# Low halves of sixteen weight loads per mixer computed on GpSimd instead of VectorE

## The chip, the cores and the metric

The kernel runs on one core of one Trainium2 chip. The metric is device time in microseconds (us); the time of a kernel is the median of its runs. In the rows of the profile PE is TensorE's matmuls and PEld its weight loads, DVE is VectorE, ACT is ScalarE, POOL is GpSimd, SP is SyncE.

## The reference, cut to what matters

Two layers of a trunk over 640 tokens (128 prompt, 512 sample) with a width of 1024. Each layer is a mixer and then a SwiGLU. The mixer is one projection `h @ w_in` that feeds three groups of heads, then `w_out`:

```python
sc_b, sc_c, sc_h, q, k, v, dn_qkv, dn_z, dn_a, dn_b = jnp.split(h @ p['w_in'], splits, axis=-1)
y_sc = sc_b * _dwconv(sc_c * sc_h, p['sc_conv_w'])
... = attention(q, k, v)
... = delta_mixer(silu(dwconv(dn_qkv)), dn_z, dn_a, dn_b)
y = jnp.concatenate([y_sc, y_att, y_dn], axis=-1) @ p['w_out']
```

The delta mixer inverts a unit lower triangular matrix for each chunk of 64 tokens and then scans over the chunks.

## The kernel before

All products take their operands as a high and a low part. `load_w` (L177) brings a slice of weights from memory into a tile `raw` (three buffers), then `split` (L170) makes two tiles of it: `whi`, a copy rounded to the matmul's type, made by ScalarE (L172), and `wlo = raw - whi`, made by VectorE (L173). Both have two buffers, so that the tiles of a load can be written once the products of the load before the last have read theirs. A product (`fm_product`, L193, and `tm_product`, L608) issues three matmuls for each slice of 128 rows: high by high (L199, L616), high by low (L201, L618), and low by high (L202, L617). The first matmul with `wlo` is thus the second or third of the product. `split` stands under `high_priority`, which lets the program's builder put both halves ahead of other work on their engines as soon as their inputs are there. Each engine then runs its instructions in the order that was fixed when the program was built.

One mixer has, in the order of its loads: two loads made before it begins (`first`), two z tiles of their own (not `whi` and `wlo`), and then sixteen loads of 128x1024 into `whi` and `wlo`: the delta mixer's n4, n5 and n0, the short convolution's c0, the delta mixer's n1, both halves of the first queries (q0a, q0b), the convolution's h0, both halves of the second queries (q1a, q1b), the convolution's b0, c1 and h1, both halves of keys and values (ka, kb), and the convolution's b1. The letters of `SEQ` set the order of the blocks: `n` is a delta mixer projection, `d` a step of the convolution, `q` queries, `k` keys and values, `I` and `J` the inversion of the large group of chunks, `i` that of the small one, `s` a scan step.

The inversion `I` is a loop of 31 steps on VectorE: `tmp <- Ls, Ts` (L999) and `Ts <- Ts, tmp` (L1001). It is followed by transposes on VectorE (L1008 to L1011), copies (`adx`, L1018) and small matmuls (L1025). GpSimd does small things in a mixer: fills, `scp * csb` of the convolution (L1138), the rotary products (L1098) and the scan's `Sd` (L1255).

Of the kernel before, what the change touches and what calls it, by code (L numbers as in the profile page):

```python
# [23 lines left out]
KT_ = 8  # L24
# [84 lines left out]
def hybrid_trunk_kernel(  # L109
# [8 lines left out]
    V, A, G, PE = nc.vector, nc.scalar, nc.gpsimd, nc.tensor  # L118
# [20 lines left out]
    def pmm():  # L139
        return ps.tile([128, 512], F32, tag="mm", name="pmm", bufs=2)  # L140
# [29 lines left out]
    def split(src, hi, lo, hi_eng=None, lo_eng=None):  # L170

        (hi_eng or A.copy)(hi, src)  # L172
        (lo_eng or V).tensor_tensor(out=lo, in0=src, in1=hi.bitcast(F32), op=ALU.subtract)  # L173

    loads = []

    def load_w(src, nk, n, side=None):  # L177
        raw = wp.tile([128, nk, n], F32, tag="raw", name="raw", bufs=RAW_BUFS)
        loads.append(nc.sync.dma_start(out=raw, in_=src))
        if isinstance(side, tuple):  # L180
            hi, lo = side
        elif side is None:
            hi, lo = (wp.tile([128, nk, n], F32R, tag=tag, name=tag, bufs=W_BUFS) for tag in ("whi", "wlo"))
        else:
            hi, lo = (side.tile([128, nk, n], F32R, tag=tag, name=tag, bufs=SIDE_BUFS) for tag in ("xhi", "xlo"))
        with tc.high_priority():
            split(raw, hi, lo)
        return hi, lo

    def wslice(w, k0, nk, c0, n):  # L190
        return w[k0 * 128:(k0 + nk) * 128, c0:c0 + n].rearrange("(k p) n -> p k n", p=128)

    def fm_product(pt, wh, wl, acts, h, lead=False):  # L193

        n = len(acts)
        o = pt[:, 0:HH]
        for k in range(n):
            ah, al = acts[k][h]
            mm(o, lhsT=wh[:, k], rhs=ah, start=k == 0, stop=False)  # L199
            if not lead:  # L200
                mm(o, lhsT=wh[:, k], rhs=al, start=False, stop=False)  # L201
            mm(o, lhsT=wl[:, k], rhs=ah, start=False, stop=not lead and k == n - 1)  # L202
        if lead:
            for k in range(n):
                mm(o, lhsT=wh[:, k], rhs=acts[k][h][1], start=False, stop=k == n - 1)
# [354 lines left out]
    def pieces(h):  # L560

        if h == 0:
            return ((0, 128, 0), (128, HH, 128))
        return ((0, HH, HH),)
# [9 lines left out]
    def padcol(tok):  # L574

        return 1 + tok if tok < 128 else 131 + tok - 128


    def mixer(l, mp, hs, early_half, fill, first, later):
        win = w_in[l]  # L580
# [6 lines left out]
        def cvt(name, shape=(128, 644), dt=F32):  # L587
            return mp.tile(list(shape), dt, tag="cv", name=name, bufs=CV_BUFS)

        def sm(tag, name, n, bufs):  # L590
            return mp.tile([128, n], F32, tag=tag, name=name, bufs=bufs)

        def padded(name):
            p = cvt(name)
            G.memset(p[:, 0:1], 0.0)
            G.memset(p[:, 129:131], 0.0)
            G.memset(p[:, 643:644], 0.0)
            return p

        def conv3(p, w0, w1, w2, name):  # L600
            y = cvt(name, (128, 642))
            A.activation(y, p[:, 0:642], AF.Copy, scale=w0)
            V.scalar_tensor_tensor(out=y, in0=p[:, 1:643], scalar=w1, in1=y, op0=ALU.mult, op1=ALU.add)
            V.scalar_tensor_tensor(out=y, in0=p[:, 2:644], scalar=w2, in1=y, op0=ALU.mult, op1=ALU.add)
            return y
# [4 lines left out]
        def tm_product(pt, ws, t):  # L610

            ts = slice(t * 128, (t + 1) * 128)
            for k in range(KT_):
                wh, wl = ws[k // 4]
                ah, al = hs[k].hi, hs[k].lo
                mm(pt, lhsT=ah[:, ts], rhs=wh[:, k % 4], start=k == 0, stop=False)  # L616
                mm(pt, lhsT=ah[:, ts], rhs=wl[:, k % 4], start=False, stop=False)  # L617
                mm(pt, lhsT=al[:, ts], rhs=wh[:, k % 4], start=False, stop=k == 7)  # L618

        def dn_load(m):  # L620
            return load_w(wslice(win, 0, KT_, 1536 + m * 128, 128), KT_, 128)

        ws = first
        ps_ = [padded("dnp") for _ in ws]
# [495 lines left out]
        ysc = []  # L1120
        def short_conv():
            for m in range(2):
                wc = load_w(wslice(win, 0, KT_, 256 + m * 128, 128), KT_, 128)
                csb = cvt("csb", (128, TOK))
                for h in range(2):
                    pt = pmm()
                    fm_product(pt, wc[0], wc[1], hs, h)
                    A.copy(csb[:, HB[h][0]:HB[h][1]], pt[:, 0:HH])
                yield
                wh_ = load_w(wslice(win, 0, KT_, 512 + m * 128, 128), KT_, 128)  # L1130
                p = padded("scp")
                for h in range(2):
                    pt = pmm()
                    fm_product(pt, wh_[0], wh_[1], hs, h)
                    for a0, a1, tok in pieces(h):
                        pv = p[:, padcol(tok):padcol(tok) + a1 - a0]
                        A.copy(pv, pt[:, a0:a1])
                        G.tensor_tensor(out=pv, in0=pv, in1=csb[:, tok:tok + a1 - a0], op=ALU.mult)  # L1138
                y = conv3(p, vl[:, 64 + m:65 + m], vl[:, 66 + m:67 + m], vl[:, 68 + m:69 + m], "scy")
                yield  # L1140
                wb = load_w(wslice(win, 0, KT_, m * 128, 128), KT_, 128)
                ys = cvt("ysc", (128, TOK))
                for h in range(2):
                    pt = pmm()
                    fm_product(pt, wb[0], wb[1], hs, h)
                    for a0, a1, tok in pieces(h):
                        V.tensor_tensor(out=ys[:, tok:tok + a1 - a0], in0=pt[:, a0:a1],
                                        in1=y[:, padcol(tok) - 1:padcol(tok) - 1 + a1 - a0], op=ALU.mult)
                ysc.append(ys)
                yield  # L1150
# [1 line left out]
        dg = short_conv()  # L1152

        def queries(hb):
            wq = [load_w(wslice(win, kk, 4, 768 + hb * 256, 256), 4, 256) for kk in (0, 4)]
            for t in range(NT):
                pt = pmm()
                tm_product(pt[:, 0:256], wq, t)
                qv = sm("qv", "qv", 256, 2)
                A.copy(qv, pt[:, 0:256])  # L1160
                headss(qv, qss[:, t, hb * 4:hb * 4 + 4], 4)
                nc.scalar.dma_start(out=qscr[t, :, hb * 256:(hb + 1) * 256], in_=qv)
            if hb == 1:
                rsqrt_dve(qss.rearrange("p t h -> p (t h)"), NT * 8, 1.0 / 64, EPS, ((rq.rearrange("p t h -> p (t h)"), lambda y: y, 0.125),), "q")


        def keys():
            kraw = cvt("kraw", (128, NT, 128))
            kvc = sm("qv", "kvc", 256, 2)
            nc.scalar.dma_start(out=kvc[:, 0:128], in_=cache_k[0, l].rearrange("s v d -> s (v d)"))  # L1170
            nc.scalar.dma_start(out=kvc[:, 128:256], in_=cache_v[0, l].rearrange("s v d -> s (v d)"))
            put_keys(kvc[:, 0:128], KTs[:, :, :, 256:384])
            put_values(kvc[:, 128:256], 5)

            wkv = [load_w(wslice(win, kk, 4, 1280, 256), 4, 256) for kk in (0, 4)]
            for t in range(NT):
                pt = pmm()
                tm_product(pt[:, 0:256], wkv, t)
                A.copy(kraw[:, t], pt[:, 0:128])
                if t == 0:  # L1180
                    nv = sm("qv", "nv", 256, 2)
                    A.copy(nv[:, 0:128], pt[:, 128:256])
                    nc.scalar.dma_start(out=new_v[0, l].rearrange("s v d -> s (v d)"), in_=nv[:, 0:128])
                put_values(pt[:, 128:256], t)
                headss(kraw[:, t], kss[:, t], 2)
            rsqrt_dve(kss.rearrange("p t h -> p (t h)"), NT * 2, 1.0 / 64, EPS, ((rk.rearrange("p t h -> p (t h)"), lambda y: y, 1.0),), "k")
            for t in range(NT):
                kn = kraw[:, t]
                scaled(kn, rk[:, t], 2)
                if t == 0:  # L1190
                    gained(kn, 64, 2)
                    nc.scalar.dma_start(out=new_k[0, l].rearrange("s v d -> s (v d)"), in_=kn)
                    put_keys(kn, KTp)
                else:
                    rope(kn, sm("asq", "ktm", 256, 2)[:, 0:128], 1, t, 2)
                    pos = (0, 1, 3, 4)[t - 1]
                    put_keys(kn, KTs[:, :, :, pos * 128:(pos + 1) * 128])
# [680 lines left out]
```

## Time and profile before

| what | value |
|---|---|
| median of 3 runs | 1778.72 us (1776.96 to 1785.07) |
| profiled execution, its own time | 1782.25 us |
| its span, first to last instruction | 1780.5 us |
| busy: PE, DVE, ACT, POOL | 94%, 70%, 44%, 9% of the span |
| granted TensorE clock, mean | 0.974 of full speed |

Busy shares are means over the whole execution. The first mixer lies between about 60 and 400 us, the second between about 925 and 1275 us; what the change touches lies in the first two thirds of each.

### The profile page before, as it was taken

To read this page: it belongs to the slowest core of one execution; us is meant where nothing else is said; L and a number is where in the kernel's file an instruction comes from. 1 tells how busy PE (TensorE), PEld (TensorE's weight loads), DVE (VectorE), ACT (ScalarE), POOL (GpSimd) and SP (SyncE) were. 2 spreads that over 40 slices of the span, in tenths; PEclk is the share of its full clock that TensorE was granted. 3 is DMA by queue.
4 is the path that set the end of the run, shared out by engine and by line. 5 is a ranking of instruction groups with operands and counts; after the bars stand their busy time and mean duration, and the time that the engine had idled before them with its cause. 6 is when DMAs were issued, how large, how long until landed. Compare 5 with 4: busy or idle time off the path is not lost. (4 is left out here: it accounts for less than half of the span.)

```text
span 1780.5 us, 34163 instructions
## 1 busy us (share of the span) xinstructions
PE 1676.7 (94%) x13677; PEld 1497.3 (84%) x13677; DVE 1242.5 (70%) x2764; ACT 782.7 (44%) x1620; POOL 156.3 (9%) x270
## 2 busy tenths in 40 slices
PE   5998999999999999999999989999998999999998
PEld 3887875478899999999988879655888999999998
DVE  3699767665966767666677994886578766667654
ACT  3555244544643433434355442555365343434332
POOL 1111012102300000000032001120041000000000
PEclk8999999999999999999999989999999999999999
DMA  8512224555534223222232222445722222222212
GB/s 280 187 37 78 72 87 129 185 178 164 155 119 131 81 74 96 72 83 73 71 99 75 63 58 67 151 143 164 233 63 84 83 73 82 83 84 84 73 59 60
DMA packets 207693, 188.42 MB, mean 106 GB/s; under 512 B 12782, under 2 KB 182702, under 8 KB 207534
## 3 DMA queue, kind: packets, MB, share of 16 engines
q1 hardware_dynamic: 190656, 170.71, 31.2%
q10 hardware_dynamic: 16878, 15.53, 2.8%
q8 instruction: 108, 1.77, 0.4%
q14 instruction: 51, 0.42, 0.1%
HBM read 168.64 MB, written 17.56 MB: 105 GB/s over the span
## 5 line engine op out<-in xcount | busy, mean ns | idle before, releaser
L172 ACT CAST whi<-raw 128x1024 fp32r<-128x1024 f32 (+1 forms) x102 | 100.0, 981 | 166.5 <-PE pmx L201 73.5
L173 DVE TENSOR_TENSOR wlo<-raw,whi 128x1024 fp32r<-128x1024 f32 (+1 forms) x102 | 115.9, 1138 | 26.5 <-ACT whi L172 26.0
L202 PE MATMUL pmm<-hh,wlo 128*128 128x320 f32 x336 | 109.4, 327 | 6.6 <-DVE wlo L173 6.5
L199 PE MATMUL pmm<-hh,whi 128*128 128x320 f32 x336 | 109.9, 328 | 4.2 <-ACT dnp L645 2.9
L199 PE MATMUL pmm<-acth,whi 128*128 128x320 f32 x320 | 100.6, 314 | 7.3 <-DVE xt L571 7.3
L571 DVE SCALAR_TENSOR_TENSOR xt<-pmx,mod,xt 128x128 f32<-128x128 f32 (+2 forms) x168 | 68.9, 434 | 51.9 <-PE pmx L202 49.5
L201 PE MATMUL pmm<-hl,whi 128*128 128x320 f32 x320 | 104.0, 325 | 0.0
L199 PE MATMUL pmx<-acth,whi 128*128 128x320 f32 x320 | 99.8, 312 | 1.8 <-DVE xt L571 1.7
L202 PE MATMUL pmm<-acth,wlo 128*128 128x320 f32 x320 | 99.8, 312 | 0.0
L201 PE MATMUL pmx<-actl,whi 128*128 128x320 f32 x320 | 99.7, 312 | 0.0
L202 PE MATMUL pmx<-acth,wlo 128*128 128x320 f32 x320 | 99.6, 311 | 0.0
L201 PE MATMUL pmm<-actl,whi 128*128 128x320 f32 x320 | 99.5, 311 | 0.0
L571 DVE SCALAR_TENSOR_TENSOR xt<-pmm,mod,xt 128x128 f32<-128x128 f32 (+2 forms) x168 | 68.6, 433 | 36.4 <-PE pmm L202 24.4
L172 ACT CAST whi<-rawd 128x1024 fp32r<-128x1024 f32 x40 | 42.0, 1049 | 107.7 <-PE pmx L201 101.6
L372 POOL TENSOR_TENSOR acc<-acc,sq 128x320 f32<-128x320 f32 x24 | 25.8, 1077 | 611.8 <-ACT sq L371 524.5
L202 PEld LDWEIGHTS pmm<-hh,wlo 128*128 128x128 f32 x336 | 66.4, 198 | 8.2 <-DVE wlo L173 7.4
L199 PEld LDWEIGHTS pmm<-hh,whi 128*128 128x128 f32 x336 | 66.5, 198 | 6.2 <-ACT dnp L645 3.8
L617 PE MATMUL pmm<-wlo,hh 128*128 128x256 f32 x240 | 70.2, 292 | 0.5 <-DVE wlo L173 0.4
L616 PE MATMUL pmm<-whi,hh 128*128 128x256 f32 x240 | 70.2, 294 | 0.0
L618 PE MATMUL pmm<-whi,hl 128*128 128x256 f32 x240 | 70.2, 293 | 0.0
L288 PE MATMUL pdn<-adaw,c 128*32 128x256 f32 x640 | 63.2, 396 | 6.2 <-DMA adaw<-in_ada_w_dram 6.0
L199 PEld LDWEIGHTS pmm<-acth,whi 128*128 128x128 f32 x320 | 60.7, 190 | 9.9 <-issue 7.0
(561 smaller groups left out, 5610.9 us busy)
## 6 DMA issues: line engine op xcount, KB each, us to landing
adaw<-in_ada_w_dram SPq DMA_DIRECT2D x80, 512.0 KB, 4.0
raw<-in_w_down_dram SPq DMA_DIRECT2D x44, 512.0 KB, 3.5
raw<-in_w_in_dram SPq DMA_DIRECT2D x36, 512.0 KB, 4.5
rawo<-in_w_gate_dram SPq DMA_DIRECT2D x40, 256.0 KB, 3.4
rawd<-in_w_gate_dram SPq DMA_DIRECT2D x40, 256.0 KB, 3.4
rawo<-in_w_up_dram SPq DMA_DIRECT2D x40, 256.0 KB, 3.4
rawd<-in_w_up_dram SPq DMA_DIRECT2D x40, 256.0 KB, 3.4
araw<-in_ada_w_dram SPq DMA_DIRECT2D x16, 512.0 KB, 6.4
```

The costliest lines, as they stand in the source:

```text
L172: (hi_eng or A.copy)(hi, src)
L173: (lo_eng or V).tensor_tensor(out=lo, in0=src, in1=hi.bitcast(F32), op=ALU.subtract)
L199: mm(o, lhsT=wh[:, k], rhs=ah, start=k == 0, stop=False)
L201: mm(o, lhsT=wh[:, k], rhs=al, start=False, stop=False)
L202: mm(o, lhsT=wl[:, k], rhs=ah, start=False, stop=not lead and k == n - 1)
L288: mm(pr[32 * q:32 * q + 32, 0:256], lhsT=c32[:, k], rhs=raw[:, q * 256:(q + 1) * 256], start=k == 0, stop=k == 7)
L372: (G if k < 5 else V).tensor_tensor(out=self.acc[h], in0=self.acc[h], in1=sq, op=ALU.add)
L571: V.scalar_tensor_tensor(out=x[:, sl], in0=pt[:, a0:a1], scalar=gate[:, g:g + 1], in1=x[:, sl], op0=ALU.mult, op1=ALU.add)
L616: mm(pt, lhsT=ah[:, ts], rhs=wh[:, k % 4], start=k == 0, stop=False)
L617: mm(pt, lhsT=ah[:, ts], rhs=wl[:, k % 4], start=False, stop=False)
L618: mm(pt, lhsT=al[:, ts], rhs=wh[:, k % 4], start=False, stop=k == 7)
```

## The change

`load_w` takes an engine for the low half and hands it to `split`. Sixteen loads of each mixer, all from the third on, pass GpSimd; the two loads of `first`, the z tiles, `w_out` and the SwiGLU keep VectorE.

```diff
-    def load_w(src, nk, n, side=None):
+    def load_w(src, nk, n, side=None, lo_eng=None):
...
-            split(raw, hi, lo)
+            split(raw, hi, lo, lo_eng=lo_eng)
...
         def dn_load(m):
-            return load_w(wslice(win, 0, KT_, 1536 + m * 128, 128), KT_, 128)
+            return load_w(wslice(win, 0, KT_, 1536 + m * 128, 128), KT_, 128, lo_eng=G)
...
-                wc = load_w(wslice(win, 0, KT_, 256 + m * 128, 128), KT_, 128)
+                wc = load_w(wslice(win, 0, KT_, 256 + m * 128, 128), KT_, 128, lo_eng=G)
...
-                wh_ = load_w(wslice(win, 0, KT_, 512 + m * 128, 128), KT_, 128)
+                wh_ = load_w(wslice(win, 0, KT_, 512 + m * 128, 128), KT_, 128, lo_eng=G)
...
-                wb = load_w(wslice(win, 0, KT_, m * 128, 128), KT_, 128)
+                wb = load_w(wslice(win, 0, KT_, m * 128, 128), KT_, 128, lo_eng=G)
...
-            wq = [load_w(wslice(win, kk, 4, 768 + hb * 256, 256), 4, 256) for kk in (0, 4)]
+            wq = [load_w(wslice(win, kk, 4, 768 + hb * 256, 256), 4, 256, lo_eng=G) for kk in (0, 4)]
...
-            wkv = [load_w(wslice(win, kk, 4, 1280, 256), 4, 256) for kk in (0, 4)]
+            wkv = [load_w(wslice(win, kk, 4, 1280, 256), 4, 256, lo_eng=G) for kk in (0, 4)]
```

## Rows read from the trace of the kernel before

**Rows 1.** The page, part 1: busy time, share and instructions of each engine.

```profile
PE 1676.7 (94%) x13677; PEld 1497.3 (84%) x13677; DVE 1242.5 (70%) x2764; ACT 782.7 (44%) x1620; POOL 156.3 (9%) x270
```

**Rows 2.** Busy time by stretch: length, PE, PEld, DVE, ACT, POOL, clock, DMA, GB/s.

```profile
60.00:210.00 150.00, 133.78 (x1312) 122.19 (x1311) 130.60 (x340) 71.95 (x146) 17.09 (x46) 0.95 0.25 70
210.00:255.00 45.00, 42.51 (x428) 39.14 (x427) 23.99 (x68) 15.05 (x39) 7.34 (x15) 1.00 0.19 55
```

**Rows 3.** Groups of VectorE's instructions, 60 to 255 us: busy us, mean ns | idle before.

```profile
L173 DVE TENSOR_TENSOR wlo<-raw,whi 128x1024 fp32r<-128x1024 f32 x16 | 19.4, 1220 | 7.5 <-ACT whi L172 7.4
...
L999 DVE TENSOR_TENSOR tmp<-Ls,Ts 128x31 f32<-128x31 f32 (+15 forms) x31 | 10.5, 340 | 0.5
```

**Rows 4.** TensorE's waits in the first, then the second mixer: us, times, longest.

```profile
PE pmm L202 <- DVE wlo L173: 4.0, 2, 2.0
...
PE pmm L202 <- DVE wlo L173: 2.5, 1, 2.5
```

**Rows 5.** GpSimd's two-input instructions at L455 and L1138: ns min/median/max, shapes.

```profile
L455 POOL TENSOR_TENSOR hl<-t,hh x12: 859/882/1102, 36.1 to 927.9; 128x320 fp32r<-128x320 f32 x12
...
L1138 POOL TENSOR_TENSOR scp<-scp,csb x12: 457/526/1468, 166.8 to 1095.0; 128x128 f32<-128x128 f32 x4, 128x192 f32<-128x192 f32 x4, 128x320 f32<-128x320 f32 x4
```

**Rows 6.** VectorE in order of time: start us, length us, what, idle before.

```profile
113.33 1.22 DVE L173 TENSOR_TENSOR wlo<-raw,whi 128x1024 fp32r<-128x1024 f32 x1 [0.82 <-ACT whi L172]
...
123.45 1.23 DVE L173 TENSOR_TENSOR wlo<-raw,whi 128x1024 fp32r<-128x1024 f32 x1
...
159.33 1.23 DVE L173 TENSOR_TENSOR wlo<-raw,whi 128x1024 fp32r<-128x1024 f32 x1
...
167.40 1.24 DVE L880 STREAM_TRANSPOSE Ls<-Ld 64x1024 f32<-64x1024 f32 x1 [1.48 <-ACT Ld L875]
...
171.09 0.22 DVE L889 TENSOR_TENSOR Ts<-Ts,tmp 128x30 f32<-128x30 f32 x1
...
171.34 0.75 DVE L887 TENSOR_TENSOR tmp<-Ls,Ts 128x56 f32<-128x56 f32 x1
...
197.02 2.35 DVE L173 TENSOR_TENSOR wlo<-raw,whi 128x1024 fp32r<-128x1024 f32 x2
...
222.67 1.23 DVE L173 TENSOR_TENSOR wlo<-raw,whi 128x1024 fp32r<-128x1024 f32 x1 [5.02 <-ACT whi L172]
```

**Rows 7.** GpSimd in order of time, first mixer.

```profile
166.79 0.94 POOL L1138 TENSOR_TENSOR scp<-scp,csb 128x128 f32<-128x128 f32 x2 [4.72 <-ACT scp L1137]
...
171.27 0.75 POOL L1138 TENSOR_TENSOR scp<-scp,csb 128x320 f32<-128x320 f32 x1 [3.44 <-ACT scp L1137]
...
223.04 1.47 POOL L1138 TENSOR_TENSOR scp<-scp,csb 128x320 f32<-128x320 f32 x1 [3.54 <-ACT scp L1137]
...
246.69 0.61 POOL L1255 TENSOR_TENSOR Sd<-S,eTs 128x256 f32<-128x256 f32 x1 [15.54 <-DVE S L1266]
```

**Rows 8.** ScalarE in order of time: the high halves of h0, b0, kb, b1.

```profile
155.09 1.03 ACT L172 CAST whi<-raw 128x1024 fp32r<-128x1024 f32 x1
...
193.77 1.05 ACT L172 CAST whi<-raw 128x1024 fp32r<-128x1024 f32 x1 [0.61 <-PE pmm L618]
...
221.59 1.05 ACT L172 CAST whi<-raw 128x1024 fp32r<-128x1024 f32 x1 [2.88 <-PE pmm L201]
...
239.75 1.05 ACT L172 CAST whi<-raw 128x1024 fp32r<-128x1024 f32 x1 [0.80 <-PE pmm L618]
```

**Rows 9.** TensorE in order of time: around the products of h0, b0, kb, b1.

```profile
157.19 0.25 PE L1025 MATMUL pkq<-adx,MK 32*32 32x32 f32 x4 [3.40 <-DVE adx L1018]
...
160.61 0.63 PE L202 MATMUL pmm<-hh,wlo 128*128 128x320 f32 x1 [2.00 <-DVE wlo L173]
...
198.29 0.41 PE L202 MATMUL pmm<-hh,wlo 128*128 128x320 f32 x1 [2.00 <-DVE wlo L173]
...
224.31 0.28 PE L617 MATMUL pmm<-wlo,hh 128*128 128x256 f32 x1
...
242.11 0.42 PE L202 MATMUL pmm<-hh,wlo 128*128 128x320 f32 x1
```

## The prediction, made before the changed kernel was run

> **What bounds the kernel now.** I read the page's busy shares first. TensorE is busy for 94% of the span, VectorE for 70% and GpSimd for 9% [rows 1]. Read alone this says that VectorE's work is covered and that GpSimd has room. These are means, so the next view is the busy time by stretch, over the part of a mixer in which the sixteen loads lie. From 60 to 210 us the order is another: VectorE is busy for 130.60 of 150 us and TensorE for 133.78, so TensorE stands idle for 16.2 us; from 210 to 255 us VectorE is busy for 23.99 of 45 us only, and TensorE for 42.51 [rows 2]. The first stretch is bound by VectorE as much as by TensorE, the second by TensorE alone. The second mixer repeats the pattern, and every term below is counted twice.
>
> The groups of VectorE's instructions say what the change takes away: sixteen low halves of 1220 ns, 19.4 us, with 7.4 us of idle time in front of them in which VectorE waited for the high half [rows 3]. Then the waits: TensorE waits for a low half twice in the first mixer, 4.0 us, and once in the second, 2.5 us [rows 4]. So 19.4 us of work lie there, but TensorE sees few of them directly. The rest of the gain, if there is any, has to come from VectorE's own chain getting shorter.
>
> **The change part by part.** *Removed from VectorE:* 16 x 1.22 us in each mixer. *Added to GpSimd:* sixteen subtractions of 128x1024. The trace has none of that width there. The nearest row is the same kind of subtraction at 128x320, 859 ns at its fastest; products of 128x128 and 128x192 have 457 and 526 ns, the minimum and the median of L1138 [rows 5]. By proportion the wide one takes 859 x 3.2 = 2.75 us, the upper end. With the slope of the two narrow ones, 69 ns for 64 elements or 1.08 ns each, it takes 859 + 704 x 1.08 = 1.62 us, the lower end. I take 2.4 us, nearer to the upper end, because the row of the same operation gives 2.7 ns an element, and only a fixed part of some 0.3 us (457 - 128 x 1.08) can be taken off it. So a low half gets 1.2 us longer, 0.4 to 1.5 by the two ends. The Trainium skill has a price too (GPSIMD Engine Reference, section 3.1, Elementwise): 4497 ns for a two-input addition of 2048 f32 elements, by which half as many would take an estimated 2.2 us; the sums below would be 0.2 us better for each low half that counts.
>
> *The two engines get in each other's way.* At 171.34 us a VectorE product of 128x56, whose neighbour takes 0.22 us, takes 0.75 us [rows 6]; it began 0.07 us after a GpSimd product of 0.75 us, and both end together at 172.0 to 172.1 [rows 7]. The other way round, GpSimd's product at 223.04 takes 1.47 us where the same one at 171.27 took 0.75, and it lies under VectorE's low half from 222.67 to 223.90 [rows 6, 7]. So an instruction of VectorE with two inputs in SBUF and one of GpSimd take turns. A transpose does not take part: the one at 167.40 takes 1.24 us though GpSimd's second product (526 ns, as elsewhere) runs until 167.73 [rows 5 to 7]. The Trainium skill states the same as a rule (SBUF — State Buffer, section SBUF: two separate sides): the pair of ports that VectorE and GpSimd share is locked for a whole instruction, and the loser stands still. The trace agrees by the 0.75 us; by that rule a low half is not taken off VectorE in a stretch of two-input work, it is replaced by a longer hold.
>
> *Term 1, the inversion loop.* Five low halves lie between 103 and 147 us, n0, c0, n1, q0a and q0b, amid the 31 steps of L999 and L1001 (10.5 us for L999 alone [rows 3]), all with two inputs in SBUF; those at 113.33 and 123.45 are two of them [rows 6]. n0 lies over copies and transposes and gains its 1.22 us. For the other four VectorE saves 1.22 and stands for up to 2.4: a loss of 4 x 1.2 = 4.7 us, less the 0.82 us for which VectorE waited for a high half at 113.33 [rows 6]. Sum: the loop ends 4.7 - 0.8 - 1.2 = 2.7 us later (by the ends -0.4 to +4.1).
>
> *Term 2, h0.* After the loop come transposes, `adx`, and TensorE's L1025, which waited 3.40 us for it at 157.19; then TensorE waited another 2.00 us for the low half of h0 [rows 9], because VectorE came to it only at 159.33, 3.2 us after the high half was done at 156.12 [rows 6, 8]. On GpSimd it is done at 156.12 + 2.4 = 158.5. If the queue of TensorE keeps its order, L1025 starts at 159.9, the 1.4 us of work between it and the wait follow, and the product resumes at 161.3 instead of 160.61: +0.7 us. If the product is put ahead of L1025, as its inputs now are there first, it runs at 158.6: -2.0 us, the whole wait. I take the middle, -0.6. The two low halves that leave VectorE here (2.45 us) give back what the loop lost, and those after it (q1b) lose 1.2 again, under TensorE's own work.
>
> *Term 3, b0.* High half done at 194.82, low half on VectorE at 198.2 behind transposes, TensorE waits 2.00 us [rows 6, 8, 9]. On GpSimd it is done at 197.2: -1.0 us, at most -1.8.
>
> *Term 4, kb.* The high half is done at 222.64 and TensorE wants the low half at 224.31 [rows 8, 9]. On VectorE it was ready at 223.90; on GpSimd it is at 225.0, +0.7. It also meets the product `scp` at 223.04 on GpSimd's queue [rows 7], which the convolution and, behind it in VectorE's queue, a scan step wait for. Whichever goes first, the other is late by 0.7 to 1.9 us (0.75 and 2.4 less the slack). I take +1.0; with the fast end of GpSimd it is 0.
>
> *Term 5, b1.* High half done at 240.80, TensorE's first use at 242.11, right behind VectorE's low half [rows 8, 9]. On GpSimd it is done at 243.2: +1.1 us (0.35 to 1.5).
>
> *At nothing:* q0b comes up to 1.2 us later for TensorE, covered by the 3.40 us that TensorE waits for `adx` afterwards [rows 9]; without that cover it would cost its 1.2. For the other loads the two buffers let a load be split while the whole product before it runs, and 1.2 us hide under those matmuls. `raw` is free 1.2 us later too; three buffers cover that, since no wait for `raw` stands in these rows.
>
> Sum for a mixer: -0.6 - 1.0 + 1.0 + 1.1 = +0.5 us; for both +1.0. The sum stands against the profiled execution's own time: 1782.25 + 1.0 = 1783.3 us. That execution is 3.5 us above the median of 1778.72, so the forecast is 1780 us. With all upper ends it is +2.1 - 0.6 + 1.9 + 1.5 = 4.9 in a mixer, 1788; with all lower ends -2.0 - 1.8 + 0 + 0.35 = -3.5, 1772. That is the forecast's own range.
>
> **The rivals.** *A, faster: VectorE is what bounds the first stretch, and the turns cost little.* Ten low halves leave VectorE between 60 and 210 us, 12.2 us in a mixer, and TensorE's 16.2 us of idle time have room for it. If GpSimd gets its turn mostly in gaps, transposes and PSUM work, some 6 to 9 of the 12.2 come back: 1761 to 1767 us. For it speaks that VectorE is busy for 130.60 of 150 us; against it the 0.75 us for a product of 0.22. It decides if a low half on GpSimd costs VectorE under about 0.5 us.
>
> *B, slower: a low half stands behind a waiting instruction on GpSimd.* GpSimd runs in order, and it waits long: `Sd` at 246.69 stood 15.54 us for a scan step [rows 7], from 231 us, across the moment (240.80) at which b1's low half becomes ready. If the program has them in the other order, b1's product waits some 6 us. One such place in each mixer costs 12 us: 1791 us. Against it speaks that the halves have priority when the order is made; it decides from the first product that waits over 4 us for GpSimd.
>
> *C: the change does nothing on the path,* because VectorE and TensorE cover it all: 1779 us, within the forecast.
>
> **How the numbers follow.** No change that a measurement of this kernel can tell is within 0.5%, 8.9 us. The forecast (C with it) gets 0.60, A 0.19, B 0.21. Of the forecast 0.53 lies within 0.5%, 0.02 below and 0.05 above; of A 0.15 is faster and 0.04 within; of B 0.17 is slower and 0.04 within. That makes 0.17 faster, 0.61 the same, 0.22 slower. For 8 in 10 the range goes from 1765, inside A, to 1791, B's time.
>
> **What would show it.** L173 on GpSimd with a median of 2.1 to 2.75 us; a VectorE L999 or L1001 stretched to over 1 us beside each of them; no wait of TensorE at the low half of b0 over 1.5 us; new waits of about 1 us at kb and b1. VectorE's busy time would fall by less than 2 x 19.4 us, since a stretched instruction counts as busy. The forecast is wrong if the loop's steps keep their 0.4 us beside GpSimd's work (A), or if GpSimd's low half begins more than 2 us after the high half's end (B).

## The result, and the profile after

The changed kernel takes 1826.14 us (median of 5 runs, 1820.4 to 1826.56) against 1778.72 us before (5 runs, 1776.96 to 1785.07): ratio 1.0256, 95% interval 1.0233 to 1.0279. It is slower by 2.6%, some 46 us; the forecast was 1780 us, with a range to 1791. The profiled execution has a span of 1824.1 us, 43.6 us more than that of before.

The page's busy times, which answer to [rows 1]:

```profile
PE 1689.9 (93%) x13677; PEld 1508.9 (83%) x13677; DVE 1267.3 (69%) x2732; ACT 782.7 (43%) x1620; POOL 233.3 (13%) x302
```

VectorE has 32 instructions fewer, 32 x 1.22 = 39 us of work that left it, and yet its busy time rose by 24.8 us. So the instructions that stayed became longer by about 64 us.

The busy time by stretch of the changed kernel, first the two stretches of [rows 2], then the two mixers, from the high half of n4 to the last product with b1:

```profile
60.00:210.00 150.00, 122.55 (x1138) 112.00 (x1138) 127.10 (x297) 66.23 (x135) 40.61 (x51) 0.91 0.21 60
210.00:255.00 45.00, 40.42 (x410) 37.88 (x409) 24.52 (x48) 12.85 (x28) 16.99 (x17) 1.00 0.26 76
61.40:276.40 215.00, 181.06 (x1734) 165.62 (x1733) 164.62 (x390) 85.85 (x184) 63.30 (x77) 0.94 0.21 60
950.90:1169.80 218.90, 186.06 (x1736) 169.62 (x1735) 167.48 (x389) 85.31 (x182) 63.56 (x77) 0.91 0.20 59
```

The same two stretches of work in the kernel before:

```profile
61.00:255.40 194.40, 175.69 (x1735) 160.54 (x1733) 154.07 (x406) 86.01 (x184) 24.43 (x61) 0.96 0.24 67
930.80:1127.40 196.60, 180.18 (x1738) 163.34 (x1739) 154.03 (x406) 85.74 (x182) 25.21 (x61) 0.94 0.23 66
```

The third column is TensorE, the one before the last two the granted clock. The two stretches are longer by 20.6 and 22.3 us, 42.9 of the 43.6 us of the span, so next to nothing of it lies elsewhere. Of the 42.9 us, 31.7 are time in which TensorE stands idle (length less busy: 33.9 and 32.8 us after, 18.7 and 16.4 before). The other 11.2 us are the same matmuls taking longer, at a granted clock of 0.94 and 0.91 where it was 0.96 and 0.94.

What stretched, by groups, 60 to 280 us. VectorE's costliest groups and one small one (L999 answers to [rows 3]), then GpSimd's low halves:

```profile
L1001 DVE TENSOR_TENSOR Ts<-Ts,tmp 128x31 f32<-128x31 f32 (+15 forms) x31 | 14.9, 481 | 0.7
L999 DVE TENSOR_TENSOR tmp<-Ls,Ts 128x31 f32<-128x31 f32 (+15 forms) x31 | 12.8, 413 | 0.7
L1242 DVE TENSOR_TENSOR sr<-vv,st 64x256 f32<-64x256 f32 x6 | 8.1, 1342 | 0.2
...
L229 DVE TENSOR_TENSOR rsw<-rsz,rsy 128x16 f32<-128x16 f32 (+3 forms) x18 | 7.1, 396 | 0.3
```

```profile
L173 POOL TENSOR_TENSOR wlo<-raw,whi 128x1024 fp32r<-128x1024 f32 x16 | 39.2, 2455 | 74.9 <-ACT whi L172 44.7 <-issue 30.1
```

The stretch is not spread over a group. It sits in single instructions that began beside a low half. VectorE in order of time, then GpSimd, first mixer:

```profile
129.84 2.62 DVE L999 TENSOR_TENSOR tmp<-Ls,Ts 128x255 f32<-128x255 f32 x1
132.49 0.42 DVE L1001 TENSOR_TENSOR Ts<-Ts,tmp 128x255 f32<-128x255 f32 x1
...
140.05 2.48 DVE L1001 TENSOR_TENSOR Ts<-Ts,tmp 128x231 f32<-128x231 f32 x1
...
170.99 2.24 DVE L229 TENSOR_TENSOR rsw<-rsz,rsy 128x16 f32<-128x16 f32 x1
173.26 2.33 DVE L231 SCALAR_TENSOR_TENSOR rsy<-rsw,rsy 128x16 f32<-128x16 f32 x1
```

```profile
129.77 2.41 POOL L173 TENSOR_TENSOR wlo<-raw,whi 128x1024 fp32r<-128x1024 f32 x1 [8.92 <-ACT whi L172]
...
139.78 2.50 POOL L173 TENSOR_TENSOR wlo<-raw,whi 128x1024 fp32r<-128x1024 f32 x1 [7.50 <-ACT whi L172]
...
170.84 4.71 POOL L173 TENSOR_TENSOR wlo<-raw,whi 128x1024 fp32r<-128x1024 f32 x2 [3.02 <-ACT whi L172]
```

The step at 129.84 began 0.07 us after the low half and took 2.62 us where its neighbour takes 0.42. At 170.99 a product of 128x16, 0.17 us by itself, takes 2.24, and the next one 2.33: the two low halves of h0 and q1a each cost VectorE a whole turn in a chain of the smallest instructions there are. Subtract from each VectorE instruction the median of the same line and shape before, and sum what is over 0.1 us. That gives 81.7 us after and 24.3 before; 53.8 us of it lie beside the 32 low halves, 1.7 us for each.

Where TensorE pays. Its waits in the first mixer, 60 to 280 us (the second repeats them, with 10.7 us at L661 and 4.6 us at L841):

```profile
PE pmx L661 <- DVE dny L657: 10.9, 5, 3.8
PE pkq L841 <- DVE MQ L846: 4.7, 1, 4.7
PE pmm L202 <- POOL wlo L173: 3.5, 3, 1.3
PE pmx L813 <- DVE qd L808: 3.2, 1, 3.2
```

The same two waits in the first mixer of the kernel before, 60 to 257 us; it has none at L841:

```profile
PE pmx L813 <- DVE qd L808: 2.6, 1, 2.6
PE pmx L661 <- DVE dny L657: 1.7, 2, 1.4
```

For low halves TensorE waits 3.5 us at L202, less than the 4.0 of [rows 4]; one more wait, of 1.4 us, is q0b's at L617, where it was 0.2. That is 4.9 us against 4.2 (in the second mixer 4.9 against 2.7), of 15.2 us that TensorE stands idle longer. The loss is in waits for ordinary results of VectorE: the delta mixer's convolution (`dny`, L603 to L657, which TensorE transposes at L661) with 9.2 us more than before, the masks at L846 with 4.7, the normalised queries at L808 with 0.6. The 3.40 us at L1025 [rows 9] are gone. TensorE in order of time, which answers to [rows 9]:

```profile
160.81 1.33 PE L661 MATMUL pmx<-ident,dny 128*128 128x128 f32 x5 [3.81 <-DVE dny L657]
...
171.34 0.57 PE L1025 MATMUL pkq<-adx,MK 32*32 32x32 f32 x42
...
173.25 0.41 PE L202 MATMUL pmm<-hh,wlo 128*128 128x320 f32 x1 [1.34 <-POOL wlo L173]
...
215.97 0.41 PE L202 MATMUL pmm<-hh,wlo 128*128 128x320 f32 x1 [1.09 <-POOL wlo L173]
...
263.41 0.41 PE L202 MATMUL pmm<-hh,wlo 128*128 128x320 f32 x1 [1.07 <-POOL wlo L173]
```

h0's product with the low half begins at 173.25 instead of 160.61, b0's at 215.97 instead of 198.29, b1's at 263.41 instead of 242.11: late by 12.6, 17.7 and 21.3 us, although the waits for the halves themselves are short.

And the clock. Two stretches of the changed kernel that begin with such waits of TensorE, and the one behind the second:

```profile
71.00:76.00 5.00, 4.62 (x21) 4.65 (x22) 3.41 (x9) 2.27 (x8) 1.01 (x4) 0.50 0.57 157
...
161.00:166.00 5.00, 5.00 (x25) 5.00 (x25) 4.88 (x7) 3.60 (x7) 1.20 (x1) 0.50 0.00 1
166.20:171.20 5.00, 5.00 (x43) 4.95 (x42) 4.71 (x17) 3.29 (x7) 1.48 (x3) 1.00 0.21 66
```

After TensorE had stood 3.81 us for L657, the next 5 us of matmuls ran at a granted clock of 0.50, its lower level of 1.2 GHz: 25 of them, where the 5 us behind, at 1.00, have 43. The stretch at 71 us follows a wait of 3.29 us.

### The profile page after: what moved, and what is told of

The parts are those of the page before. It is cut to its first block, busy times and chain, and to the rows that moved or that the text cites. A ratio compares the mean times of both kernels' runs of the same rounds, so it can differ in the third digit from the quotient of the medians.

```text
span 1824.1 us, 34165 instructions
## 1 busy us (share of the span) xinstructions
PE 1689.9 (93%) x13677; PEld 1508.9 (83%) x13677; DVE 1267.3 (69%) x2732; ACT 782.7 (43%) x1620; POOL 233.3 (13%) x302
## 5 line engine op out<-in xcount | busy, mean ns | idle before, releaser
L202 PE MATMUL pmm<-hh,wlo 128*128 128x320 f32 x336 | 107.6, 322 | 7.0 <-POOL wlo L173 7.0
L202 PE MATMUL pmm<-acth,wlo 128*128 128x320 f32 x320 | 99.5, 311 | 0.0
L202 PE MATMUL pmx<-acth,wlo 128*128 128x320 f32 x320 | 99.2, 310 | 0.0
L173 POOL TENSOR_TENSOR wlo<-raw,whi 128x1024 fp32r<-128x1024 f32 x32 | 78.3, 2452 | 153.9 <-ACT whi L172 93.1
L173 DVE TENSOR_TENSOR wlo<-raw,whi 128x1024 fp32r<-128x1024 f32 (+1 forms) x70 | 77.1, 1101 | 13.2 <-ACT whi L172 12.8
L616 PE MATMUL pmm<-whi,hh 128*128 128x256 f32 x240 | 75.1, 313 | 3.1 <-ACT qv L1160 3.1
L617 PE MATMUL pmm<-wlo,hh 128*128 128x256 f32 x240 | 74.4, 310 | 2.7 <-POOL wlo L173 2.7
L618 PE MATMUL pmm<-whi,hl 128*128 128x256 f32 x240 | 73.9, 308 | 0.0
L202 PEld LDWEIGHTS pmm<-hh,wlo 128*128 128x128 f32 x336 | 65.0, 194 | 8.8 <-POOL wlo L173 8.3
```

## The experiments

Two theories at first. *Turns*: GpSimd's subtraction makes VectorE stand, and VectorE's ordinary results come late. *Late halves* (rival): the low half itself is done 1.2 us later, and that is what delays TensorE. A third, *order*: the order of the instructions, fixed when the program is built, came out worse. The edits below are shown against the changed kernel, one line of each.

The table holds every run. "Stretch" is the sum over VectorE's instructions as worked out above, from the profiled execution (24.3 before). "Span x clock" is the mean over the executions of span times mean granted clock, so an estimate of the time it would take if the withheld clock were given back; the kernel before has 1731.2 to 1731.4 in it, at a mean clock of 0.9746 to 0.9754, in the three comparisons with 20 or 25 executions of it, and 1731.1 at 0.9743 in the one with 7 (pieces).

| kernel | low halves on GpSimd | median, us | ratio to before, 95% interval | stretch, us | span x clock, us | clock |
|---|---|---|---|---|---|---|
| changed | 32 | 1826.14 | 1.0256 (1.0233 to 1.0279) | 81.7 | 1760.0 | 0.966 |
| dummy | 32, unread | 1833.5 | 1.0313 (1.0284 to 1.0342) | 80.1 | 1759.0 | 0.9605 |
| memset | fills only | 1772.48 | 0.9966 (0.9951 to 0.9981) | 35.1 | 1730.4 | 0.9779 |
| copy1 | 32 copies | 1780.07 | 1.0018 (0.9996 to 1.0040) | 41.7 | 1735.5 | 0.9758 |
| g_dn | 8 | 1784.63 | 1.0037 (1.0019 to 1.0055) | 38.5 | 1736.5 | 0.9738 |
| g_conv | 12 | 1794.5 | 1.0086 (1.0055 to 1.0116) | 44.9 | 1739.3 | 0.9708 |
| g_loop | 10 | 1786.55 | 1.0050 (1.0029 to 1.0070) | 42.0 | 1743.6 | 0.977 |
| g_rest | 22 | 1807.59 | 1.0162 (1.0113 to 1.0211) | 64.8 | 1739.9 | 0.964 |
| g_wait | 4 | 1774.98 | 0.9987 (0.9965 to 1.0009) | 28.7 | 1731.1 | 0.9763 |
| g_first | 4 | 1781.01 | 1.0007 (0.9989 to 1.0025) | 30.1 | 1733.2 | 0.9746 |
| g_q1 | 4 | 1779.28 | 1.0007 (0.9994 to 1.0021) | 31.6 | 1731.8 | 0.9741 |
| g_tail | 10 | 1790.83 | 1.0075 (1.0053 to 1.0097) | 41.5 | 1736.5 | 0.9701 |
| pieces | 32 x 4 | 1807.56 | 1.0162 (1.0121 to 1.0203) | 63.1 | 1757.6 | 0.9738 |

**The suspected cost without the change: dummy.** VectorE makes all low halves, GpSimd repeats the sixteen subtractions into a tile that nothing reads.

```diff
-            split(raw, hi, lo, lo_eng=lo_eng)
+            split(raw, hi, lo); lo_eng and lo_eng.tensor_tensor(out=scratch[-1].rearrange("p (k n) -> p k n", k=nk), in0=raw, in1=hi.bitcast(F32), op=ALU.subtract)
```

> VectorE makes every low half as in the kernel before; GpSimd makes the same sixteen subtractions of each mixer once more into a scratch tile that nobody reads. Theory T (turns: each subtraction of 2.4 us on GpSimd holds the access to SBUF that VectorE's two-input instructions need, so VectorE stands for about 2 us each time): VectorE gets no relief and loses some 30 x 2 us, so its busy time rises by 50 to 60 us, and the time by 30 to 60 us over before (1810 to 1840 us). Rival R (the products wait for a low half that comes 1.2 us later): nothing waits for the scratch tile, so under 5 us over before. Rival O (the loss comes from the new order of the queues, not from the turns): VectorE's work and so its order stay nearly as before, so under 10 us.

It is as slow as the change and more, 1.0313. VectorE in order of time, and GpSimd beside it:

```profile
129.22 0.41 DVE L999 TENSOR_TENSOR tmp<-Ls,Ts 128x240 f32<-128x240 f32 x1
129.60 1.23 DVE L173 TENSOR_TENSOR wlo<-raw,whi 128x1024 fp32r<-128x1024 f32 x1
130.74 2.62 DVE L1001 TENSOR_TENSOR Ts<-Ts,tmp 128x240 f32<-128x240 f32 x1
```

```profile
130.04 3.05 POOL L187 TENSOR_TENSOR scratch<-raw,whi 128x1024 bf16<-128x1024 f32 x1 [7.46 <-DVE tmp L999]
```

No low half comes from GpSimd here, and VectorE's other 2622 instructions stand in the order of before, all but 12 of them. The loss comes all the same: halves made later by GpSimd, and the order, fall as its main cause, and the turns are shown. VectorE's own low halves do come late, because VectorE stands: in the first mixer TensorE waits 9.9 us for them (5.4 at L202, 4.5 at L617) instead of 4.2, which is 5.7 us of some 21 that it stands idle longer. The unread subtraction takes 3.05 us there, from inside VectorE's own low half to near the end of VectorE's next step: either engine stands for the other.

**The change without the turns: memset.** GpSimd only writes the low tiles, twice, so that they are ready about as late.

```diff
-            split(raw, hi, lo, lo_eng=lo_eng)
+            split(raw, hi, lo) if lo_eng is None else (A.copy(hi, raw), G.tensor_copy(lo[:, 0, 0:1], hi[:, 0, 0:1].bitcast(F32)), G.memset(lo.bitcast(F32), 0.0), G.memset(lo.bitcast(F32), 0.0))
```

> The sixteen low halves of each mixer are not computed: GpSimd reads one column of the high half, so that it waits for it, and then fills the low half with zeros twice (2 x 0.96 us by the fills of the kernel before), an instruction without an input in SBUF. VectorE is relieved as in the change, the low half comes about as late as in the change (some 2.1 us after the high half), but no turns are taken. T: the loss goes and the relief stays, so at or below the kernel before: 1755 to 1782 us. R: the late low halves still cost 8 to 10 us: 1787 us or more. O: the order of the queues changes as in the change, so 1800 us or more.

0.9966. GpSimd's group, 60 to 260 us, and three of VectorE's instructions beside fills (121.56 to 123.53 and 155.35 to 157.33 us):

```profile
L187 POOL MEMSET wlo<- 128x1024 f32 x32 | 30.5, 954 | 1.6
```

```profile
121.84 0.43 DVE L1001 TENSOR_TENSOR Ts<-Ts,tmp 128x255 f32<-128x255 f32 x1
122.30 0.42 DVE L999 TENSOR_TENSOR tmp<-Ls,Ts 128x256 f32<-128x256 f32 x1
...
155.35 1.09 DVE L875 COPY Ld<-MK 32x128 f32<-32x128 f32 x1
```

Two-input steps keep their 0.42 us beside a fill; the copy of 32x128, 0.28 to 0.30 us elsewhere, does not. Two things follow. Halves that come 2.5 us after the high half (the median), as late as in the changed kernel, cost nothing net. And the whole relief of VectorE by 39 us is worth 6 us, 0.34%: that is the prize for which the change was in the running at all, and it lies in the clock (0.9779), since span x clock stays within 1 us of before. In span x clock dummy, the turns without the change, has 27.6 us over before, and memset, the change without the turns, has 1.0 under it; together 26.6 of the changed kernel's 28.7.

**One input in place of two: copy1.**

```diff
-            split(raw, hi, lo, lo_eng=lo_eng)
+            split(raw, hi, lo) if lo_eng is None else (A.copy(hi, raw), G.tensor_copy(lo, raw))
```

> GpSimd copies raw into the low tiles (one input read from SBUF, so the tiles hold the whole weight and not the low part: the output is not the reference's) in place of the subtraction with two. If it is GpSimd's second input that makes the two engines take turns, VectorE's stretch stays near that of the fills (35 us) and the time near theirs, ratio 0.995 to 1.000. If any GpSimd instruction that reads SBUF takes turns, the stretch goes by its length: at 1.2 to 2.4 us each, 50 to 80 us of stretch and ratio 1.01 to 1.025.

1.0018, no difference that can be told. The stretch is 41.7 us, 17 over before's, 15.1 of it beside copies that take 36.6 us in sum; so copies take turns as well; the first branch of the expectation, that only a second input does it, falls, and the numbers of the second were too high, because a copy takes 1.14 us on average. VectorE, then GpSimd:

```profile
122.55 1.22 DVE L999 TENSOR_TENSOR tmp<-Ls,Ts 128x252 f32<-128x252 f32 x1
```

```profile
122.45 1.04 POOL L187 CAST wlo<-raw 128x1024 fp32r<-128x1024 f32 x1 [7.98 <-PE pmm L202]
```

The step again stands until GpSimd is done, 0.80 us longer than alone, as the step at 129.84 us of the changed kernel stood 2.20. With turns of 1.04 instead of 2.4 us the stretch over before's is 17 us instead of 57, and the relief of VectorE pays for most of it.

Copy1 also says more of the order than dummy does. Low halves aside, its 2622 instructions of VectorE stand in the order of the changed kernel, all but 8; the changed kernel itself has 207 out of the order of before. TensorE's waits, copy1, 60 to 260 us:

```profile
PE pmx L661 <- DVE dny L657: 8.1, 5, 3.8
PE pkq L841 <- DVE MQ L846: 6.5, 1, 6.5
```

So the longest waits at L661 and L841 come with this order, and a kernel that has them need not be slower: copy1 is 4.2 us over before in span x clock, the changed kernel 28.7.

**By group of loads: g_dn and g_conv.** `lo_eng=G` stands only at the delta mixer's loads (g_dn: n4, n5, n0, n1) or only at the convolution's (g_conv: c0, h0, b0, c1, h1, b1).

```diff
-            wc = load_w(wslice(win, 0, KT_, 256 + m * 128, 128), KT_, 128, lo_eng=G)
+            wc = load_w(wslice(win, 0, KT_, 256 + m * 128, 128), KT_, 128)
```

> Only the delta mixer's loads (n4, n5, n0, n1, 8 of 32 low halves) on GpSimd, the other 24 on VectorE. T: n5, n0 and n1 fall into two-input work and lose 1 us each net, so 4 to 10 us over before (1783 to 1789). R: none of their products waits for the low half, so no change within 2 us. O: if the order of the inversion's stretch is what costs, most of the 45 us is here: 1800 us or more.

> Only the short convolution's loads (c0, h0, b0, c1, h1, b1, 12 of 32 low halves) on GpSimd. T: 12 x 1 us net, less the waits of TensorE behind transposes (h0, b0) that go: 0 to 12 us over before. R: the three products that wait (h0, b0, b1) cost or give back about 1 us each: within 4 us of before. O: 1790 us or more.

1.0037 and 1.0086: each group costs something, so it is no single place. g_dn came as the turns had it; g_conv's 1794.5 us lies over their 0 to 12 us and in what I had written down for the order (1790 or more). By this run alone the order could be the cause there; dummy and copy1 speak against it. g_conv's profiled execution (1785.58 us) lies 9 us below its median.

**Term 1 by itself, and all the others: g_loop and g_rest.** g_loop has n0, c0, n1, q0a and q0b on GpSimd, g_rest the other eleven.

```diff
-            return load_w(wslice(win, 0, KT_, 1536 + m * 128, 128), KT_, 128, lo_eng=G)
+            return load_w(wslice(win, 0, KT_, 1536 + m * 128, 128), KT_, 128, lo_eng=G if m < 2 else None)
```

> Low halves of n0, c0, n1, q0a and q0b alone on GpSimd (10 of 32), those beside the loop of 31 steps. This is Term 1 by itself. Prediction's Term 1: +2.7 us for a mixer, +5.4 us in all, ratio 1.003, with VectorE's stretch some 10 us above before's 24. Turns (T): in the changed kernel these ten stretched VectorE's instructions by 19 us and TensorE's first use of the tiles fell behind by some 6 to 8 us more over that stretch, so +10 to +18 us, ratio 1.006 to 1.010, stretch 40 to 45 us.

> The other 22 of 32 on GpSimd: n4, n5, h0, q1, b0, c1, h1, keys and values, b1. The prediction costs these at -0.9 us or less for a mixer (its Terms 2 to 5, with no loss from the loop to hand on): about -2 us, ratio 0.999. Turns (T): they stretched VectorE by about 40 us in the changed kernel, so +25 to +35 us, ratio 1.014 to 1.020, and with g_loop the two excesses add up to about the whole 47 us.

g_loop's 1.0050 lies between the two expectations (+5.4 and +10 to +18 us): some 9 us. g_rest has 1.0162, within the range by the turns, where the prediction's terms say a small gain. By time most of the loss thus comes with these eleven loads, seven of them put at nothing and four (h0, b0, kb, b1) priced. By kind the two differ: of g_rest's excess 8.6 us are span x clock and 21.2 withheld clock (span less span x clock), of g_loop's 12.3 and -2.7. The two ratios sum to 2.12% of the 2.56, not to the whole as I had expected.

**Only the two halves that TensorE waited for: g_wait**, with h0 and b0.

```diff
-            wh_ = load_w(wslice(win, 0, KT_, 512 + m * 128, 128), KT_, 128, lo_eng=G)
+            wh_ = load_w(wslice(win, 0, KT_, 512 + m * 128, 128), KT_, 128, lo_eng=None if m else G)
```

> Only the low halves of h0 and b0 on GpSimd (4 of 32), the two that TensorE waited 2.0 us for because VectorE was behind transposes and copies. Prediction's Terms 2 and 3 without the loop's loss: 1.5 to 2.0 and 1.0 us earlier for a mixer, about -5 us in all, ratio 0.997. Turns (T): the waits shrink to 1.3 and 1.1 us as in the changed kernel (-3 us in all), and 2 to 4 us of stretch beside h0 and 0.9 beside b0 take it back: ratio 0.998 to 1.002.

0.9987, not to be told from 1. VectorE's copy of `adx`, with GpSimd's low half of h0 beside it, and TensorE behind:

```profile
155.35 2.91 DVE L1018 COPY adx<-DD 32x512 f32<-32x512 f32 x2
```

```profile
155.41 2.56 POOL L173 TENSOR_TENSOR wlo<-raw,whi 128x1024 fp32r<-128x1024 f32 x1 [12.22 <-issue]
```

```profile
158.40 0.31 PE L1025 MATMUL pkq<-adx,MK 32*32 32x32 f32 x4 [5.45 <-DVE adx L1018]
```

The two copies took 0.87 us before. With one input each, they stand like a product does, and L1025 now waits 5.45 us instead of the 3.40 of [rows 9]. What TensorE gained at h0's low half it lost in front of it.

**The rest of the partition: g_first, g_q1, g_tail** (n4 and n5; q1a and q1b; c1, h1, ka, kb and b1). With g_loop and g_wait these five hold each of the 32 low halves once.

> Only n4 and n5, the first two of the sixteen loads, on GpSimd (4 of 32). The prediction puts them at nothing. Turns (T): in the changed kernel they stood in front of the convolution's steps L603 and L604 (2.1 us beside n5), and n4's own product came 4 to 5 us late in each mixer: +5 to +9 us, ratio 1.003 to 1.005.

> Only q1a and q1b on GpSimd (4 of 32). The prediction costs them at nothing, as a loss under TensorE's own work. Turns (T): beside them stand the normalisation's smallest instructions (L229, L231; 1.8 to 4.2 us of stretch for a low half), and L813 waits for their result: +4 to +10 us, ratio 1.002 to 1.006.

> Only c1, h1, ka, kb and b1 on GpSimd (10 of 32), where TensorE alone was the bound before. The prediction: kb +1.0 and b1 +1.1 us for a mixer, +4.2 us, ratio 1.0024. Turns (T): the changed kernel fell behind by 3 us a mixer over this stretch, +5 to +8 us, ratio 1.003 to 1.0045. Together with g_loop (+8.9 us) and g_wait (-2.3) the five parts hold all 32 low halves; if what each costs simply adds up, the three of this batch come to some +40 us; if they come to 20 or less, the losses add more than their sum, since each alone finds slack that all together have used up.

1.0007, 1.0007 and 1.0075. For the first two my expectation by the turns was too high, and the prediction's nothing stands; g_tail costs more than either expectation for it (1.0024, and 1.003 to 1.0045). The five parts sum to 0.50 - 0.13 + 0.07 + 0.07 + 0.75 = 1.26%, half of the 2.56% of all together. In span x clock they sum to 12.3 - 0.1 + 2.0 + 0.6 + 5.4 = 20.2 us against 28.7; in withheld clock to -2.7 - 1.7 + 0.1 + 0.9 + 8.4 = 5.0 us against 17.4. So the losses do more than add up, and the clock is the larger part of what comes on top (12.4 us, and 8.5 in span x clock).

**Shorter turns: pieces.** Each low half as four subtractions of 128x256.

```diff
-            split(raw, hi, lo, lo_eng=lo_eng)
+            split(raw, hi, lo) if lo_eng is None else (A.copy(hi, raw), [G.tensor_tensor(out=lo[:, k:k + nk // 4], in0=raw[:, k:k + nk // 4], in1=hi[:, k:k + nk // 4].bitcast(F32), op=ALU.subtract) for k in range(0, nk, nk // 4)])
```

> All sixteen low halves on GpSimd as in the changed kernel, but each as four subtractions of 128x256 (some 0.6 to 0.75 us each by the widths seen, 2.6 us for a low half) in place of one of 2.4 us. If VectorE only suffers from the length of one GpSimd instruction (it stands for what is left of it, then has its turn), the longest stretch falls from 2.2 to about 0.7 us, the sum of VectorE's stretch from 82 to 45 to 60 us, and about half of the 47 us comes back: ratio 1.010 to 1.016, with GpSimd's pieces standing in their turn behind VectorE. If the engines are held for GpSimd's whole work however it is cut, the stretch stays at 75 to 85 us and the ratio at 1.022 to 1.03.

1.0162, at the edge of the first expectation, but not for its reason. GpSimd's group, and VectorE beside one low half:

```profile
L187 POOL TENSOR_TENSOR wlo<-raw,whi 128x256 fp32r<-128x256 f32 x128 | 103.0, 838 | 137.2 <-ACT whi L187 77.8 <-issue 59.3
```

```profile
137.66 0.82 DVE L1001 TENSOR_TENSOR Ts<-Ts,tmp 128x231 f32<-128x231 f32 x1
138.52 0.81 DVE L999 TENSOR_TENSOR tmp<-Ls,Ts 128x220 f32<-128x220 f32 x1
139.37 0.81 DVE L1001 TENSOR_TENSOR Ts<-Ts,tmp 128x220 f32<-128x220 f32 x1
140.21 0.80 DVE L999 TENSOR_TENSOR tmp<-Ls,Ts 128x207 f32<-128x207 f32 x1
```

Four steps each take twice their 0.4 us: the engines alternate. The stretch falls by a third of what the change had added, to 63.1 us (45 to 60 expected), but span x clock hardly moves (1757.6 against 1760.0). What came back is withheld clock: 47.4 us on average instead of 61.9, within 2 us of the 7 executions of before in the same comparison. So the 18.6 us of the gain are the clock's for the most part; the loss itself was spread, not removed.

## Why the prediction was wrong

**What held.** GpSimd's subtraction takes 2.35 to 2.50 us in 26 of 32 places (median 2.40; I had 2.4). The two engines take turns, as read from one product of 0.75 us [rows 6, 7]. Terms 3 and 5 came out: b0's wait fell from 2.00 to 1.09 us (I had -1.0), b1's is 1.07 (+1.1). At h0 it went from 2.00 to 1.34 (-0.6 forecast), which is luck: -0.6 was the middle of two cases, both with L1025's wait for `adx`, and that wait is gone. Kb, +1.0 by Term 4, has no wait at all; its high half was not late, and 2.65 us were left. Q0b, put at nothing under the cover of L1025's 3.40 us, waits 1.35 us: the cover went with the wait. The waits for low halves grew by 0.7 us in the first mixer and 2.2 in the second, where the sum had +0.5; so what the prediction priced came out nearly as it said, and the 46 us lie elsewhere.

**Term 1** was not too small in itself. The loop's 62 steps took 21.1 us before and 27.7 after in the first mixer, and c0's low half made the convolution's L657 among them stand for 2.2; four low halves, 4.9 us, left it: +3.9 us net, where I had 4.7 before what I took off. But I charged the turns to these four only.

**The step that failed** is the one after it: that the loss of VectorE beside the other loads lies "under TensorE's own work", and the "At nothing" of the last paragraph, "1.2 us hide under those matmuls". There I asked when the low half is ready, and not what VectorE does not get done meanwhile. Hiding a late half under matmuls is right (memset: halves as late, no loss). But the VectorE instruction that stands for up to 2.4 us is not the half's; it belongs to whatever chain is running, and that chain can end at TensorE: n5's low half (66.92 to 69.82 us) made L604 stand (2.1 us over its usual 0.88), and L661 waited 3.29 us, 1.38 before; q1b's made L229 stand (1.95 us from 181.73), at the head of the chain to L808, and L813 waited 3.20, 2.58 before. Sixteen low halves in a mixer cost VectorE 27 us, not the 4 x 2.4 that I counted, and return 19.5. g_rest alone, for which my terms gave no loss, costs 1.6%. One such wait is not yet a loss: in g_first L661 waits 3.31 us at the same place, in g_q1 L813 waits 4.04, and neither kernel is slower by more than its interval. So what "at nothing" had wrong is the whole and not each part; that each delay by itself finds slack further on, and all together use it up, is how I read the sums over the five parts above, and no run traces it.

A smaller error in the same place: I let copies off ("n0 lies over copies and transposes and gains its 1.22 us"). Transposes and reductions do go on: in g_wait, beside 2.4 us of GpSimd, L900 and L901 take 2.1 to 2.2 us, and in the first mixer of the changed kernel n0's low half, beside transposes, stretches nothing. Copies do not: 2.05 us of stretch at L1018 in g_wait, 3.2 us at L987 beside n0 in the second mixer. The Trainium skill says which do (SBUF — State Buffer, section Who interferes with whom): copies and single-input tensor_scalar operations that can take both ports contend with any GpSimd instruction, two inputs in SBUF only with one that reads SBUF, a reduction never. The runs agree in each: in memset fills leave the loop's steps at 0.42 us, stretch a copy to 1.09 and a tensor_scalar (L221, 128x16) from 0.17 to 1.00, and L1067's reductions stay at 0.50 us or less beside fills and at 0.42 beside subtractions.

**What the sum lacked** is the clock. I priced idle time of TensorE at its length. In the changed kernel 11.2 us of the 42.9 are matmuls behind such waits at the lower level; by the executions' mean, 17.4 us of clock were withheld on top of before's 44.6.

**The order**, too, has a part that I can place but not price. In the changed kernel n1's convolution stands behind the loop and among the transposes:

```profile
151.29 0.19 DVE L1001 TENSOR_TENSOR Ts<-Ts,tmp 128x31 f32<-128x31 f32 x1
...
152.07 2.14 DVE L1008 STREAM_TRANSPOSE DD<-Ts 64x1024 f32<-64x1024 f32 x1
154.10 0.85 DVE L603 SCALAR_TENSOR_TENSOR dny<-dnp,vec,dny 128x642 f32<-128x642 f32 x1
...
159.96 0.80 DVE L657 SCALAR_TENSOR_TENSOR dny<-dnp,dny 128x642 f32<-128x642 f32 x1
```

That is the wait of 3.81 us at L661. Its input was there at 147.97 us (ScalarE's L602), four us before L1008 began, so a queue that ran it first would not have waited as long; before, it ran inside the loop. L841's 4.69 us are of the same kind: its mask (L846) stands behind the last step of the small group's loop. Memset has both, and there the loop really is short (29.7 us against 38.4; 37.5 before) and the waits are 2.20 and 4.0 us, paid for by the 39 us that left VectorE. Here nearly the same order met a VectorE that had more to do, not less. Dummy, with the order of before, loses as much, and copy1, with this order and waits of 3.82 and 6.5 us, hardly loses, so this does not decide the result; why the parts in span x clock sum to 20.2 and not 28.7 us stays open.

**The rivals.** A, faster: its condition, under 0.5 us of VectorE for a low half, is far from met (1.7 us), and its prize was wrong too: thirteen low halves lie between 60 and 210 us, not the ten that I counted, and still memset gives 6 us for nearly free low halves and not 12 to 18. B, slower by a low half behind a waiting GpSimd instruction: no product waits over 1.35 us for GpSimd. B ended on the right side for a cause that isn't the one seen.

None of these kernels is worth having for its speed: the only faster one computes no low halves.

## What to carry to other kernels

Moving elementwise work from VectorE to GpSimd takes it off VectorE only in part, and here not at all: an instruction of 2.4 us on GpSimd stopped VectorE for 1.7 us on average, to save 1.2. Count every instruction that is moved, whether its own result is urgent or not, and ask which chain VectorE is in at that moment and when TensorE wants its end; a cover found for the result does not cover the neighbour. Price a new wait of TensorE with what the clock does behind it, and do not take the costs of single moves for the cost of all: here the parts summed to half.

## What the runs showed of the hardware that was not expected

- The smallest two-input instruction stands a whole turn: 128x16, 0.17 us alone, 2.24 us beside a subtraction of 2.36.
- Executions of one kernel differ largely by the clock: before went from 1770.33 us (clock 0.978) to 1786.19 (0.973) in one comparison of 25. The means over 20 or 25 executions lie up to 1.3 us apart in span (1775.0 to 1776.3) and 0.2 in span x clock (1731.2 to 1731.4).
- A copy from f32 on GpSimd is over twice as fast as the subtraction: 1.04 us against 2.35 for 128x1024, and a fill 0.95; the subtraction in quarters takes 0.71 each at its fastest.
